# Placing ScalarE's share of a recurrence, a pooling stage's first splits and a w_a operand by ordering edges

## The chip, the cores and the metric

The kernel runs on one NeuronCore of a Trainium2 chip. The metric is the device time of one execution in microseconds (us), from start to end. Five engines work beside each other, each through its own instructions in order: TensorE (PE, with its weight loads shown as PEld), VectorE (DVE), ScalarE (ACT), GpSimd (POOL), and SyncE (SP), which here only issues DMA transfers. A time of this kernel is told apart from another when the two differ by about 0.2%, or 3 us.

## What is computed

One decoder block on 1024 tokens of width 1024, in float32. Its core, cut from the reference:

```python
proj = x @ w_in                     # -> q | f | i | og | pool_v | gate_a | gate_b, 1024 columns each
f = lb + (1 - lb) * sigmoid(f_pre);  k = 1 - f;  q = silu(q) * 128 ** -0.5
# per head of 128:  S_t = diag(f_t) S_{t-1} + k_t i_t^T,   o_t = S_t^T q_t
o = o * rsqrt(mean(o ** 2) + eps) * hgrn_norm_g * sigmoid(og)
a = o @ w_a
b = per_group_linear(causal_mean_w(pool_v) - pool_v, w_pool) * pool_scale
x = LN(alpha * x + (sigmoid(gate_a) * a + sigmoid(gate_b) * b) @ w_out)
x = LN(alpha * x + relu(x @ w_up) ** 2 @ w_down)
```

## The kernel before

**Products.** Every large product is cut Strassen-fashion into seven products of halves of 512 (`pair`, L267). One such product is 12 matmuls of 128x512 (`prod`, L207 to L215): four pieces of the contraction, each with high by high (L212), high by low (L214) and low by high (L215), because each operand is held as a high and a low part. A weight tile `raw` that DMA brought is split when it is needed: ScalarE writes the high part `w<-raw` (L126), VectorE subtracts it for the low one (L127). Results collect in four PSUM banks `ps_pj`; a bank is given back when ScalarE has copied it (`copied`, L275, into a tile `c`, `f` or `q`) or VectorE has added it (`added`, L279). Sigmoids of gates and of recurrence inputs (L690, L697, L717, L733) are ScalarE's too.

**The recurrence.** Between 115 us and 600 us the products of `x @ w_in` run, and the recurrence of eight heads in two halves of 512 tokens runs beside them. TensorE's order is fixed by hand there (`ORDER`, L33, and `turning`, L377): behind each product the recurrence takes one turn, 8.25 turns for one of the 16 halves. In the first turn of a half stand the outputs of the half before (L1025, L1027), and on ScalarE their squares (L1031), a root (L1032, which loads a function table first) and four scalings by it (L1035); then the transposed keys (L964, their copy L966) and the scores of this half (L971, L982) in the PSUM bank `sc`. In the turns behind it the next half is prepared by pieces (`prepare`, L890): running products on VectorE (L897 to L905), k = 1 - f on ScalarE (L909), products on VectorE (L935, L937), two ScalarE copies (L940, L943) with VectorE's other halves of them, three VectorE products (L946 to L949), and two more ScalarE copies (L953, L955) into `q64` and `k64`, which the last scores (L982) read. In the fourth turn the scaled outputs are transposed (L1041).

**The pooling stage and w_a.** When the recurrence's inputs are all made, the loop over `POOL_AFTER` (L1096) sets the pooling's products (`pool_products`, L746; L113 to L115 in one of two banks `ps_tr`) between the products of the last two gate pairs. w_pool's four groups are loaded into one tile `tC` (L763) in turn and split (L768) into `tD`, `tE`, `tF` and `og`, their inputs `po` in L769. For each product a gate tile `f<-gb` is loaded (ring of four tiles, L784), multiplied with the bank (L791) and stored as `pb<-f` (L792); the last two instead are copied out by ScalarE (L789). Then comes `a = o @ w_a`: `o_operand` (L628) loads four tiles `c<-o` for "a11" (L635) and splits each (ScalarE L131, VectorE L132).

**Who sets the order.** TensorE's is written out in this stretch; the order of ScalarE, VectorE, GpSimd and SP is chosen when the program is built, by a scheduler that simulates the engines. `tc.issue_after(x)` gives it an ordering edge: what is issued inside goes behind x on x's own engine, or behind x's issue, without a semaphore.

Of the kernel before, what the change touches and what calls it, by code (L numbers as in the profile page):

```python
# [28 lines left out]
NW = 10  # L29
PER_HALF = 8.25  # L30
TURN_BACK = 4
TURNS_AHEAD = 3
ORDER = (  # L33
    ("inputs", 1), ("pooled", 0), ("inputs", 2), ("gates", 0), ("output_gates", 2), ("inputs", 3), ("pooled", 1),
# [17 lines left out]
def tile_hybrid_block(  # L52
# [189 lines left out]
    def w_tile():  # L242
        return wq.tile([P, CH, P], F32R, tag="w", name=nm("w"), bufs=NW)

    def w_part(src):
        return split(src, w_tile)

    n_c = [0]

# [17 lines left out]
    def pair(raw, rooms, takes, pz_tag="pj", twin=False, pc_tag="pj", turned=False):  # L267
# [4 lines left out]

        def copied(room, ps):
            t = room()
            A.copy(t, ps)  # L275
            return t

        def added(t, ps):
# [375 lines left out]
    with tc.tile_pool(name="tmp", bufs=1, side="right", reuse_waits="tile") as tmp:  # L654
# [25 lines left out]
        def head_inputs(h, behind=()):  # L680
            fs, qs = inputs[h] = [None, None], [None, None]

            def room_f():
                fs[1] = tt("f")
                return fs[1]

            def take_f(u):
                def take(src):
                    t = fs[u] = fs[u] or tt("f")
                    A.activation(t, src, AF.Sigmoid)  # L690
                    A.activation(t, t, AF.Identity, bias=lb[:, h : h + 1], scale=one_lb[:, h : h + 1])
                return take

            def take_q(u):
                def take(src):
                    t = qs[u] = tt("q")
                    A.activation(t, src, AF.Sigmoid)  # L697
# [14 lines left out]
        def output_gates(h):  # L712

            def take(dst, src=False):
                def put(t):
                    s = c_late() if src else t
                    A.activation(s, t, AF.Sigmoid)  # L717
                    nc.sync.dma_start(out=dst, in_=s)
                return put

            run(pair(
                loaded_blocks(w_in, 3 * D + h * P, 3 * D + (h + 1) * P), (c_soon, c_late, c_late),
                (take(ogd[h][0]), take(ogd[h + 1][0], True), take(ogd[h][1]), take(ogd[h + 1][1])),
            ))

        def gates(j):
            final = j == KT - 1
            room = (lambda: tt("q")) if final else c_late

            def take(dst, src=None, u=None):  # L730
                def put(t):
                    s = (tt("og") if final else c_late()) if src else t
                    A.activation(s, t, AF.Sigmoid)  # L733
# [10 lines left out]
        held = [None, None]  # L744

        def pool_products():  # L746

# [16 lines left out]
                return raw, [loaded(pod[2 * g + i][u], pod_tile) for i in range(2)]  # L764

            def parts(g, u, raw, pods):
                if raw is not None:
                    w_parts[g] = split(raw, lambda: wide(w_tiles(F32R)))  # L768
                return [split(t, row_tile) for t in pods]  # L769

            w_parts = {}
            todo = [(g, u) for g in range(CH) for u in range(2)]
# [3 lines left out]
            for n, (g, u) in enumerate(todo):  # L776
                if n + 2 < len(todo):
                    soon.append(load(*todo[n + 2]))
                wh, wl = w_parts[g]
                for i in (0, 1) if g < CH - 1 else (1, 0):  # L780
                    w = slice(i * P, (i + 1) * P)
                    j = 2 * g + i
                    final = j == KT - 1
                    t = tt("v") if final else loaded(gbd[j][u], lambda: tt("f"))  # L784
                    ps = ps_tile("tr", 2)
                    mm3(ps, [(wh[:, c, w], wl[:, c, w], *pl[c]) for c in range(2)])
                    if final:
                        held[u] = t
                        A.activation(t, ps, AF.Copy, scale=pscale[:, j : j + 1])  # L789
# [95 lines left out]
        class Half:  # L885
# [4 lines left out]
            def prepare(self):  # L890
# [14 lines left out]
                V.tensor_tensor_scan(  # L905
                    to_end[:, QUARTER - 1 :: -1], ft[:, QUARTER : 0 : -1], first_of, 0.0, ALU.mult, ALU.max,
                )
                k = ft
                A.activation(k, ft, AF.Identity, bias=cmask[:, P - 1 : P], scale=-1.0)  # L909
# [23 lines left out]
                G.tensor_mul(ek[:, :, 0], p64[:, :, 1], p32[:, :, 1])  # L933
                yield
                V.tensor_mul(q, q, fd)  # L935
                self.kr = kr = tt("tE")
                V.tensor_mul(kr, k, to_end)  # L937
                yield
                self.kc = kc = tt("tD")
                A.copy(pairs_of(kc)[:, :, 0], pairs_of(kr)[:, :, 0])  # L940
                V.tensor_mul(pairs_of(kc)[:, :, 1], pairs_of(kr)[:, :, 1], bc(rT2[:, :, 1], [P, NB // 2, SUB]))
                self.qc = qc = tt("tF")
                A.copy(pairs_of(qc)[:, :, 1], pairs_of(q)[:, :, 1])  # L943
# [6 lines left out]
                yield  # L950
                self.q64 = q64 = hgp.tile([P, CH, 2, 32], F32, tag="q64", name=nm("q64"))
                self.k64 = k64 = hgp.tile([P, CH, 2, 32], F32, tag="k64", name=nm("k64"))
                A.copy(q64[:, :, 0], half64(q, 1)[:, :, 0])  # L953
                V.tensor_mul(q64[:, :, 1], half64(q, 1)[:, :, 1], bc(p32[:, :, 2], [P, CH, 32]))
                A.copy(k64[:, :, 1], half64(kr, 0)[:, :, 1])  # L955
                V.tensor_mul(k64[:, :, 0], half64(kr, 0)[:, :, 0], bc(p32[:, :, 1], [P, CH, 32]))
                self.q = q

# [60 lines left out]
            def outputs(self):  # L1019
# [11 lines left out]
                    A.activation(on[:, chunk(c)], o[:, chunk(c)], AF.Square, accum_out=ss[:, c : c + 1])  # L1031
                A.activation(ss, ss, AF.Sqrt, bias=eps_rms, scale=1.0 / P)  # L1032
                V.reciprocal(ss, ss)
                for c in range(CH):
                    A.activation(on[:, chunk(c)], o[:, chunk(c)], AF.Copy, scale=ss[:, c : c + 1])  # L1035

            def turn_outputs(self):

# [7 lines left out]
        def recurrence():  # L1046
# [10 lines left out]
            for n in range(2 * HEADS + 1):  # L1057
# [483 lines left out]
```

## Time and profile before

| | |
|---|---|
| median of 3 runs | 1460.81 us (1459.44 to 1462.52) |
| the profiled execution | 1460.42 us |
| its span, first to last instruction | 1458.7 us (1.7 us lie outside it) |
| granted TensorE clock, mean | 0.996 |
| VectorE busy | 1100.4 us (75%) |
| ScalarE busy | 759.3 us (52%) |
| chain of work that ended last | PE 86%, DVE 7%, DMA 3%, ACT 2% |
| 115 to 600 us: TensorE busy | 478.13 of 485.00 us |
| 600 to 665 us: TensorE busy | 59.08 of 65.00 us, DMA share 0.87 |
| 665 to 850 us: TensorE busy | 185.00 of 185.00 us |

How to read it: a row of a timeline has the start, the duration, the engine, the line of the kernel, the operation, what it writes and reads, and in brackets the idle time of the engine ahead of it with what ended that. Matmuls are pipelined, so one of 128x512 lasts 0.39 us and the next starts 0.227 us behind it. A view of waits lists, for each waiting line, what it waited for, the total in us, the number of times and the longest.

### The profile page before, as it was taken

What the parts mean: (1) busy time and instruction counts of PE and PEld (TensorE: products, weight loads), DVE (VectorE), ACT (ScalarE), POOL (GpSimd) and SP (SyncE); (2) the same over time, 40 slices, a digit from 0 to 9 for tenths busy, and PEclk for the clock granted to TensorE, in tenths of its full rate; (3) what the DMA queues carried; (4) which work ended last, traced back from release to release, by engine and by line L of the source; (5) the groups of instructions that cost most, each with busy time, mean ns of one, the idle gap of its engine ahead of it and who ended that gap; (6) DMA issues with size and microseconds to landing.
All of it is one profiled execution on the core that took longest, in us unless ns stands there. A gap on an engine that the chain in (4) does not pass through costs nothing.

```text
span 1458.7 us, 20882 instructions
## 1 busy us (share of the span) xinstructions
PE 1433.3 (98%) x7377; PEld 1188.7 (81%) x7377; DVE 1100.4 (75%) x1807; ACT 759.3 (52%) x1383; POOL 106.7 (7%) x288
## 2 busy tenths in 40 slices
PE   9999999999999999989999999999999999999997
PEld 7888888888887887868888888888888888888886
DVE  6968878888697795579885598666666787777877
ACT  5445567566656655556442366555555443333535
POOL 0002112112212110000002100000000100000000
PEclk9999999999999999999999999999999999999999
DMA  7242344444454455689463125444447774445322
GB/s 267 65 130 88 99 125 138 123 112 143 110 133 127 123 132 169 192 315 354 135 231 111 68 92 188 158 144 154 146 162 262 281 253 156 148 141 171 121 73 115
DMA packets 187161, 228.15 MB, mean 156 GB/s; under 512 B 12176, under 2 KB 110512, under 8 KB 187056
## 3 DMA queue, kind: packets, MB, share of 16 engines
q1 hardware_dynamic: 181088, 212.91, 44.0%
q0 software_dynamic: 5184, 11.54, 4.1%
q10 hardware_dynamic: 784, 2.38, 0.5%
q8 instruction: 58, 0.95, 0.3%
q14 instruction: 47, 0.39, 0.1%
HBM read 149.70 MB, written 77.07 MB: 155 GB/s over the span
## 4 chain that ended last, share of the span: by engine, by line
PE 86%; DVE 7%; DMA 3%; ACT 2%; issue 1%; SPq 0%; DVEq 0%; ACTq 0%
PE ps_pj L212 14%; PE ps_pj L215 14%; PE ps_pj L214 14%; PE ps_pj L1423 4%; PE ps_pj L1424 4%; PE ps_pj L1422 4%; PE ps_pj L114 2%; PE ps_pj L115 2%; PE ps_pj L113 2%; PE ps_tr L1423 1%; PE ps_tr L1424 1%; PE ps_tr L1422 1%; DVE w L127 1%; PE ps_hg L212 1%; PE ps_sc L215 1%
## 5 line engine op out<-in xcount | busy, mean ns | idle before, releaser
L212 PE MATMUL ps_pj<-act,w 128*128 128x512 f32 x1068 | 422.2, 395 | 12.4 <-ACT c L275 5.6
L215 PE MATMUL ps_pj<-act,w 128*128 128x512 f32 x1068 | 416.7, 391 | 0.6 <-DVE w L127 0.6
L214 PE MATMUL ps_pj<-act,w 128*128 128x512 f32 x1068 | 416.6, 391 | 0.0
L126 ACT CAST w<-raw 128x512 fp32r<-128x512 f32 x311 | 192.9, 622 | 272.0 <-PE ps_pj L214 184.0
L127 DVE TENSOR_TENSOR w<-raw,w 128x512 fp32r<-128x512 f32 x311 | 213.0, 687 | 102.2 <-ACT w L126 100.8
L212 PEld LDWEIGHTS ps_pj<-act,w 128*128 128x128 f32 x1068 | 201.3, 188 | 58.0 <-ACT c L275 7.4
L215 PEld LDWEIGHTS ps_pj<-act,w 128*128 128x128 f32 x1068 | 201.2, 188 | 44.7 <-DVE w L127 1.8
L214 PEld LDWEIGHTS ps_pj<-act,w 128*128 128x128 f32 x1068 | 201.3, 188 | 40.7
L1384 ACT CAST act<-act 128x1024 fp32r<-128x1024 f32 x66 | 66.9, 1050 | 109.0 <-issue 35.0
L1424 PE MATMUL ps_pj<-act,act 128*128 128x512 f32 x240 | 93.0, 389 | 0.0
L1423 PE MATMUL ps_pj<-act,act 128*128 128x512 f32 x240 | 93.0, 389 | 0.0
L1385 DVE TENSOR_TENSOR act<-act,act 128x1024 fp32r<-128x1024 f32 x66 | 79.5, 1221 | 17.8 <-ACT act L1384 17.8
L1422 PE MATMUL ps_pj<-act,act 128*128 128x512 f32 x240 | 92.5, 389 | 0.0
L279 DVE TENSOR_TENSOR c<-c,ps_pj 128x512 f32<-128x512 f32 x91 | 62.1, 682 | 31.0 <-PE ps_pj L215 30.6
L275 ACT COPY c<-ps_pj 128x512 f32<-128x512 f32 x92 | 53.5, 582 | 3.0 <-PE ps_pj L215 1.7
L1422 PEld LDWEIGHTS ps_pj<-act,act 128*128 128x128 f32 x240 | 45.0, 188 | 9.4
L1423 PEld LDWEIGHTS ps_pj<-act,act 128*128 128x128 f32 x240 | 45.0, 188 | 9.4
L1424 PEld LDWEIGHTS ps_pj<-act,act 128*128 128x128 f32 x240 | 45.0, 188 | 9.3
L284 DVE TENSOR_TENSOR raw<-raw,raw 128x512 f32<-128x512 f32 x43 | 29.6, 689 | 30.5 <-DMA raw<-in_w_in_dram 28.6
L1293 ACT ACTIVATE c<-c 128x512 f32<-128x512 f32 x61 | 38.6, 633 | 1.7
L1292 ACT ACTIVATE c<-c 128x512 f32<-128x512 f32 x46 | 29.1, 632 | 15.6 <-DVE c L279 15.5
L1378 DVE TENSOR_TENSOR act<-act,ps_pj 128x512 f32<-128x512 f32 x45 | 30.2, 683 | 5.4 <-PE ps_pj L1424 5.1
(415 smaller groups left out, 2683.5 us busy)
## 6 DMA issues: line engine op xcount, KB each, us to landing
h<-c SPq DMA_DIRECT2D x106, 256.0 KB, 2.8
raw<-in_w_in_dram SPq DMA_DIRECT2D x100, 256.0 KB, 3.1
act<-h SPq DMA_DIRECT2D x78, 256.0 KB, 3.0
draw<-in_w_down_dram SPq DMA_DIRECT2D x16, 1024.0 KB, 7.8
raw<-in_w_up_dram SPq DMA_DIRECT2D x56, 256.0 KB, 2.9
hf<-h SPq DMA_DIRECT2D x34, 256.0 KB, 2.9
s<-og POOLq DMA_DIRECT2D x28, 256.0 KB, 6.2
v<-v SPq DMA_DIRECT2D x16, 256.0 KB, 3.2
```

Of the source, the lines that this page charges most:

```text
L126: A.copy(hi, src)
L127: V.tensor_sub(lo, src, f(hi))
L212: PE.matmul(ps, wh[:, k], th, start=first and k == 0, stop=False, skip_group_check=True)
L214: PE.matmul(ps, wh[:, k], tl, start=False, stop=False, skip_group_check=True)
L215: PE.matmul(ps, wl[:, k], th, start=False, stop=k == CH - 1, skip_group_check=True)
L275: A.copy(t, ps)
L279: V.tensor_add(t, t, ps)
L1384: A.copy(hi, src)
L1385: V.tensor_sub(lo, src, f(hi))
L1422: PE.matmul(ps, hh[:, w], wh, start=fresh and n == 0, stop=False, skip_group_check=True)
L1423: PE.matmul(ps, hh[:, w], wl, start=False, stop=False, skip_group_check=True)
L1424: PE.matmul(ps, hl[:, w], wh, start=False, stop=n == M - 1, skip_group_check=True)
```

## The change

1. `noted` remembers the last bank copy (`copied`) or sigmoid that was issued, and everything that the recurrence asks of ScalarE is put behind it (`behind_act`): k = 1 - f (L909), the copies of L940, L943, L953, L955, and the four scalings of L1035. k = 1 - f is also written one piece later, and the scalings become a function of their own, `scale_outputs`, which is called in the turn behind the root (`TURN_SCALE = 1`) and not with it.
2. `w_part` keeps each weight split's two instructions; `behind_weight` puts w_pool's parts and their inputs' behind the last weight split written so far.
3. The loads of operand a11 are put behind the last load of a gate tile `f<-gb`, and its splits behind the fourth last weight split.

No instruction is added or removed on any engine.

```diff
 def w_part(src):
-    return split(src, w_tile)
+    hi, lo = w_tile(), w_tile()
+    hi_of.append(A.copy(hi, src).ins)
+    lo_of.append(V.tensor_sub(lo, src, f(hi)).ins)
+    return hi, lo
+
+@contextmanager
+def behind_weight(n=-1):
+    with tc.issue_after(hi_of[n]), tc.issue_after(lo_of[n]):
+        yield
+
+def noted(i):
+    last_act[0] = i.ins
+    return i
+
+def behind_act():
+    return tc.issue_after(last_act[0])
...
-            A.copy(t, ps)
+            noted(A.copy(t, ps))
...
             def parts(g, u, raw, pods):
-                if raw is not None:
-                    w_parts[g] = split(raw, lambda: wide(w_tiles(F32R)))
-                return [split(t, row_tile) for t in pods]
+                with behind_weight():
+                    if raw is not None:
+                        w_parts[g] = split(raw, lambda: wide(w_tiles(F32R)))
+                    return [split(t, row_tile) for t in pods]
...
-                    t = tt("v") if final else loaded(gbd[j][u], lambda: tt("f"))
+                    t = tt("v") if final else tt("f")
+                    if not final:
+                        last_gate[0] = nc.sync.dma_start(out=t, in_=gbd[j][u]).ins
...
-                k = ft
-                A.activation(k, ft, AF.Identity, bias=cmask[:, P - 1 : P], scale=-1.0)
...
                 V.tensor_mul(q, q, fd)
+                k = ft
+                with behind_act():
+                    A.activation(k, ft, AF.Identity, bias=cmask[:, P - 1 : P], scale=-1.0)
...
-                A.copy(q64[:, :, 0], half64(q, 1)[:, :, 0])
+                with behind_act():
+                    A.copy(q64[:, :, 0], half64(q, 1)[:, :, 0])
...
-                for c in range(CH):
-                    A.activation(on[:, chunk(c)], o[:, chunk(c)], AF.Copy, scale=ss[:, c : c + 1])
+                self.o, self.root = o, ss
+
+            def scale_outputs(self):
+                with behind_act():
+                    for c in range(CH):
+                        w = chunk(c)
+                        A.activation(self.on[:, w], self.o[:, w], AF.Copy, scale=self.root[:, c : c + 1])
...
                 for turn in range(1, round(at) - round(at - PER_HALF)):
+                    if turn == TURN_SCALE and old:
+                        old.scale_outputs()
                     if turn == TURN_BACK:
...
-        o_operand("a11")
+        with tc.issue_after(last_gate[0]), behind_weight(-4):
+            o_operand("a11")
```

What that moves, at three places. In the rows the number behind a name tells tiles apart; lines are those of each kernel's own text (L126, L275, L909, L953, L955, L1032 and L1035 of before are L250, L294, L958, L979, L982, L1059 and L1068 after the change; L131, L789, L635 and L623 for a gate tile are L132, L811, L654 and L806).

ScalarE behind the root of the outputs at 444.76 us of the trace (`c_897` is the copy of the bank `ps_pj_883`). Before:

```order
L1032 ACT_TABLE_LOAD
L1032 ACTIVATE ss_891_4843<-ss_891_4843,eps_rms_82 128x4
L909 ACTIVATE f_873_4778<-f_873_4778,cmask_79 128x512
L1035 ACTIVATE tH_892_4844<-ps_hg_890_4835,ss_891_4843 128x128 x4
L126 COPY w_930_5056<-raw_925_5047 128x512
L275 COPY c_897_4908<-ps_pj_883_4800 128x512
```

After the change:

```order
L1059 ACT_TABLE_LOAD
L1059 ACTIVATE ss_891_4843<-ss_891_4843,eps_rms_82 128x4
L250 COPY w_930_5056<-raw_925_5047 128x512
L294 COPY c_897_4904<-ps_pj_883_4800 128x512
L1068 ACTIVATE tH_892_4844<-ps_hg_890_4835,ss_891_4843 128x128 x4
L250 COPY w_934_5078<-raw_926_5049 128x512
```

The weight's high part and the bank copy moved ahead of the scalings and of k = 1 - f, which now stands six rows behind the scalings. The same happens behind the root at 304.44 us.

ScalarE ahead of a score at 495.6 us (`q64_994` and `k64_995` are what L982 of before reads; `c_993` is the copy of bank `ps_pj_983`). Before, the two copies stood thus, some 15 rows ahead of the bank copy `c_993`:

```order
L940 COPY tD_985_5346<-tE_968_5275 128x16x16
L126 COPY w_987_5352<-raw_977_5320 128x512
L953 COPY q64_994_5393<-q_870_4756 128x4x32
L275 COPY f_952_5201<-ps_pj_936_5082 128x512
L955 COPY k64_995_5394<-tE_968_5275 128x4x32
```

After the change:

```order
L752 ACTIVATE c_984_5344<-c_984_5344 128x512
L250 COPY w_1029_5579<-raw_1024_5570 128x512
L294 COPY c_993_5391<-ps_pj_983_5331 128x512
L979 COPY q64_994_5393<-q_870_4756 128x4x32
L982 COPY k64_995_5394<-tE_968_5275 128x4x32
```

They moved behind the bank copy. VectorE's products of the same half (L946, L947, L949 and L956 of before) moved likewise, to just ahead of the addition of `c_984`.

ScalarE at 640 us (`act_1360` and `act_1362` are parts of operand a11, `v_1330` is the pooling's product `ps_tr_1331` copied out, `w_1311` a weight of the last gate pair). Before, with `v_1330` twenty-one rows behind the first of these:

```order
L131 COPY act_1360_7108<-c_1361_7109 128x512
L126 COPY w_1311_6882<-raw_1292_6820 128x512
L275 COPY q_1299_6844<-ps_pj_1298_6831 128x512
L126 COPY w_1323_6930<-tA_1301_6848 128x512
L126 COPY w_1325_6934<-tA_1302_6850 128x512
L131 COPY act_1362_7113<-c_1363_7114 128x512
```

After the change:

```order
L250 COPY w_1338_6986<-raw_1293_6822 128x512
L132 COPY act_1360_7108<-c_1361_7109 128x512
L294 COPY q_1329_6956<-ps_pj_1298_6831 128x512
L132 COPY act_1362_7113<-c_1363_7114 128x512
L811 ACTIVATE v_1330_6958<-ps_tr_1331_6959,prm_120 128x512
L132 COPY act_1364_7118<-c_1365_7119 128x512
```

The parts of a11 moved behind the split of `w_1338`, two gate products later, and two of them now stand ahead of the copying out of `ps_tr_1331`. Their loads on SP moved too. After the change SP's rows there read (`f_1343` is the last gate tile):

```order
L806 DMA f_1332_6967<-gb6_0_963 128x512
L806 DMA f_1343_7016<-gb6_1_964 128x512
L755 DMA ga7_0_949<-q_1299_6844 128x512
L654 DMA c_1361_7109<-o0_0_903 128x512
L814 DMA pb4_1_992<-f_1317_6904 128x512
L654 DMA c_1363_7114<-o1_0_905 128x512
```

Before, the load of `c_1361` stood ahead of the last six gate tiles' loads.

Likewise w_pool's first parts (`tD_1213<-tC_1208`), which stood just behind the scalings at 554.99 us, now stand behind the split of `w_1205`, which ran at 578.49 us.

More of the change, by code (lines that the diff above doesn't have):

```diff
@@ L31 @@
 TURN_BACK = 4
+TURN_SCALE = 1
 TURNS_AHEAD = 3
@@ L243, in w_tile @@
         return wq.tile([P, CH, P], F32R, tag="w", name=nm("w"), bufs=NW)
+    hi_of, lo_of, last_act = [], [], [None]
     def w_part(src):
-        return split(src, w_tile)
+        hi, lo = w_tile(), w_tile()
[11 more added lines that the diff above has]
+        return tc.issue_after(last_act[0])
     n_c = [0]
@@ L690, in take @@
                     A.activation(t, src, AF.Sigmoid)
-                    A.activation(t, t, AF.Identity, bias=lb[:, h : h + 1], scale=one_lb[:, h : h + 1])
+                    noted(A.activation(t, t, AF.Identity, bias=lb[:, h : h + 1], scale=one_lb[:, h : h + 1]))
                 return take
@@ L696, in take @@
                     t = qs[u] = tt("q")
-                    A.activation(t, src, AF.Sigmoid)
+                    noted(A.activation(t, src, AF.Sigmoid))
                     V.scalar_tensor_tensor(t, src, QSCALE, t, ALU.mult, ALU.mult)
@@ L716, in put @@
                     s = c_late() if src else t
-                    A.activation(s, t, AF.Sigmoid)
+                    noted(A.activation(s, t, AF.Sigmoid))
                     nc.sync.dma_start(out=dst, in_=s)
@@ L732, in put @@
                     s = (tt("og") if final else c_late()) if src else t
-                    A.activation(s, t, AF.Sigmoid)
+                    noted(A.activation(s, t, AF.Sigmoid))
                     if final and u is not None:
@@ L742, in gates @@
             ))
-        held = [None, None]
+        held, last_gate = [None, None], [None]
         def pool_products():
@@ L939, in prepare @@
                 self.kc = kc = tt("tD")
-                A.copy(pairs_of(kc)[:, :, 0], pairs_of(kr)[:, :, 0])
+                with behind_act():
+                    A.copy(pairs_of(kc)[:, :, 0], pairs_of(kr)[:, :, 0])
                 V.tensor_mul(pairs_of(kc)[:, :, 1], pairs_of(kr)[:, :, 1], bc(rT2[:, :, 1], [P, NB // 2, SUB]))
                 self.qc = qc = tt("tF")
-                A.copy(pairs_of(qc)[:, :, 1], pairs_of(q)[:, :, 1])
+                with behind_act():
+                    A.copy(pairs_of(qc)[:, :, 1], pairs_of(q)[:, :, 1])
                 V.tensor_mul(pairs_of(qc)[:, :, 0], pairs_of(q)[:, :, 0], bc(rT2[:, :, 0], [P, NB // 2, SUB]))
@@ L952, in prepare @@
                 self.k64 = k64 = hgp.tile([P, CH, 2, 32], F32, tag="k64", name=nm("k64"))
-                A.copy(q64[:, :, 0], half64(q, 1)[:, :, 0])
+                with behind_act():
+                    A.copy(q64[:, :, 0], half64(q, 1)[:, :, 0])
                 V.tensor_mul(q64[:, :, 1], half64(q, 1)[:, :, 1], bc(p32[:, :, 2], [P, CH, 32]))
-                A.copy(k64[:, :, 1], half64(kr, 0)[:, :, 1])
+                with behind_act():
+                    A.copy(k64[:, :, 1], half64(kr, 0)[:, :, 1])
                 V.tensor_mul(k64[:, :, 0], half64(kr, 0)[:, :, 0], bc(p32[:, :, 1], [P, CH, 32]))
@@ L1033, in outputs @@
                 V.reciprocal(ss, ss)
-                for c in range(CH):
-                    A.activation(on[:, chunk(c)], o[:, chunk(c)], AF.Copy, scale=ss[:, c : c + 1])
+                self.o, self.root = o, ss
+            def scale_outputs(self):
+                with behind_act():
+                    for c in range(CH):
+                        w = chunk(c)
+                        A.activation(self.on[:, w], self.o[:, w], AF.Copy, scale=self.root[:, c : c + 1])
             def turn_outputs(self):
```

## The prediction

> **What bounds the kernel now.** I read the page's head first, then its costliest groups, then the view of waits of TensorE, and after that timelines around each wait. Page and waits:
>
> ```profile
> span 1458.7 us, 20882 instructions
> PE 1433.3 (98%) x7377; PEld 1188.7 (81%) x7377; DVE 1100.4 (75%) x1807; ACT 759.3 (52%) x1383; POOL 106.7 (7%) x288
> ```
>
> ```profile
> PE ps_pj L212 <- ACT c L275: 5.6, 3, 3.1
> PE ps_pj L212 <- ACT w L126: 5.3, 1, 5.3
> PE ps_pj L212 <- ACT f L275: 0.8, 1, 0.8
> PE ps_pj L215 <- DVE w L127: 0.6, 2, 0.5
> PE ps_pj L212 <- DVE c L279: 0.6, 1, 0.6
> ```
>
> TensorE is busy 98% of the span. The change doesn't touch its instructions, so it can win only these waits, 5.6 + 5.3 + 0.8 + 0.6 + 0.6 = 12.9 us, and what follows a wait. ScalarE is 52% busy, so work is late there by its place in the queue and not for want of time. The question is then, for each wait, what the copy or split that ends it was queued behind, and whether the moved work is itself in time.
>
> **The change part by part.** All starts are on the trace's own time. Matmuls of a block start 0.23 us apart (635.76 and 635.99 in the rows of the stretch from 636 us), so a wait's price is the distance of the two starts around it less 0.23.
>
> *The wait at 446 us.* ScalarE, then TensorE:
>
> ```profile
> 444.76 0.30 ACT L1032 ACTIVATE ss<-ss,eps_rms 128x4 f32<-128x4 f32 x1
> 445.65 0.72 ACT L909 ACTIVATE f<-f,cmask 128x512 f32<-128x512 f32 x1 [0.59 <-DVE tC L905]
> 446.56 1.14 ACT L1035 ACTIVATE tH<-ps_hg,ss 128x128 f32<-128x128 f32 x4 [0.19 <-DVE ss L1033]
> 447.58 0.63 ACT L126 CAST w<-raw 128x512 fp32r<-128x512 f32 x1
> 448.08 0.61 ACT L275 COPY c<-ps_pj 128x512 f32<-128x512 f32 x1
> ```
> ```profile
> 446.12 0.39 PE L215 MATMUL ps_pj<-act,w 128*128 128x512 f32 x1
> 448.75 0.50 PE L212 MATMUL ps_pj<-act,w 128*128 128x512 f32 x1 [2.24 <-ACT c L275]
> 449.09 0.40 PE L214 MATMUL ps_pj<-act,w 128*128 128x512 f32 x1
> ```
>
> The bank copy ended at 448.69 and TensorE began the next block at 448.75, 448.75 - 446.12 - 0.23 = 2.4 us late, and 0.1 more at the restart. Ahead of the copy stood k = 1 - f and the scalings, both waiting for VectorE. After the change the split and the copy come right behind the root: the root ends at 445.06, the split takes about 0.5 to the next start, the copy ends at about 446.2. The bank is wanted at 446.35. **-2.5 us.** What is late next is the scalings, three rows further on; the transposes that read them (L1041) stand in the fourth turn, so they cost nothing as long as they lose under 3 us, by my reading of the order.
>
> *The wait at 308 us* is that for `f` in the view of waits, 0.8, and has the same form: the bank copy behind root, k = 1 - f and scalings. With 0.1 at the restart: **-0.9 us**.
>
> *The wait at 558 us.*
>
> ```profile
> 560.33 0.62 ACT L126 CAST tD<-tC 128x512 fp32r<-128x512 f32 x1 [4.20 <-DMA tC<-in_w_pool_dram]
> 561.37 0.58 ACT L275 COPY c<-ps_pj 128x512 f32<-128x512 f32 x1
> ```
> ```profile
> 558.47 0.39 PE L215 MATMUL ps_pj<-act,w 128*128 128x512 f32 x1
> 562.00 0.50 PE L212 MATMUL ps_pj<-act,w 128*128 128x512 f32 x1 [3.14 <-ACT c L275]
> ...
> 563.93 0.63 PE L212 MATMUL ps_pj<-act,w 128*128 128x512 f32 x1
> ...
> 566.45 0.40 PE L212 MATMUL ps_pj<-act,w 128*128 128x512 f32 x1
> ```
>
> ScalarE stood 4.20 us before w_pool's first split, for a load, with a bank copy behind it. TensorE restarts 562.00 - 558.47 - 0.23 = 3.3 us late. Then its matmuls last 0.63 us for a while and not 0.39: the twelve from 562.00 to 566.45 take 4.45 where 12 x 0.23 = 2.76 are due, 1.7 more. After the change the w_pool split stands behind a weight split that ran at about 578 us, and the bank copy behind the root, done by 556 us, where it is wanted at 558.7. The first pooling product begins at 605 us, so the split has over 20 us left. **-5.0 us.** [...] Here the rows decide: matmuls last 0.63 behind 3.14 us of idle time, and 0.40 at once behind the 2.24 us that end at 448.75.
>
> *The stretch from 636 us.* ScalarE, TensorE and SP:
>
> ```profile
> 640.46 0.62 ACT L131 CAST act<-c 128x512 fp32r<-128x512 f32 x1 [7.80 <-DMA c<-o]
> ...
> 653.98 0.69 ACT L789 ACTIVATE v<-ps_tr,prm 128x512 f32<-128x512 f32 x1
> ```
> ```profile
> 635.76 0.39 PE L114 MATMUL ps_tr<-w,tD 128*128 128x512 f32 x1
> 635.99 0.39 PE L115 MATMUL ps_tr<-w,tE 128*128 128x512 f32 x1
> 641.65 0.80 PE L212 MATMUL ps_pj<-act,w 128*128 128x512 f32 x1 [5.27 <-ACT w L126]
> 646.00 0.39 PE L113 MATMUL ps_tr<-w,tD 128*128 128x512 f32 x1
> ...
> 657.87 0.40 PE L113 MATMUL ps_tr<-w,tF 128*128 128x512 f32 x1
> ```
> ```profile
> 638.33 0.55 SPq L623 DMA_DIRECT2D f<-gb  x1
> ```
> ```profile
> f<-gb SPq DMA_DIRECT2D x14, 256.0 KB, 3.1
> pb<-f SPq DMA_DIRECT2D x14, 256.0 KB, 4.7
> c<-o SPq DMA_DIRECT2D x12, 256.0 KB, 4.7
> ```
>
> a11's first part waited 7.80 us for its load, and the weight split that TensorE needs stood behind it: 641.65 - 635.99 - 0.23 = 5.4 late, then a block of 4.35 (to 646.00) for 2.76, 1.6 more, and the 0.5 of L127's wait shortly behind: 7.5 us to win. But only if nothing takes its place before the pooling product at 657.87, which would then be due at 650.4. That product takes the bank that L789 copies out, and after the change two parts of a11 stand ahead of L789, whose loads stand behind the last gate tile's. That load is paced by its ring of four tiles: the last but four was issued at 638.33, landed 3.1 later (641.4), is multiplied in some 0.75 and stored in 4.7 (646.9), so the last can leave at about 647; the store of a gate and a11's two loads follow within 1.4 us, the second lands 4.7 later, at 653.1. Its split (0.62) and L789 (0.69) end at 654.4. The product restarts there, 657.87 - 654.4 = 3.5 earlier than before, not 7.5: **-3.5 us**. The bounds are 0, where loads land no sooner than now, and -7.5, where they land some 4 us sooner than the rows' medians. I take the rows' medians.
>
> *New waits.* VectorE first. At 404 us TensorE waits 0.6 for a bank that VectorE adds (`c` by L279 in the view of waits). VectorE's groups, with their mean duration in ns:
>
> ```profile
> L817 DVE TENSOR_TENSOR pC<-pA 128x269 f32<-128x269 f32 (+1 forms) x32 | 13.8, 430 | 0.3
> ...
> L949 DVE TENSOR_TENSOR tC<-tE,ek 128x512 f32<-128x512 f32 x16 | 10.9, 682 | 0.1
> ...
> L956 DVE TENSOR_TENSOR k<-tE,p 128x128 f32<-128x128 f32 x16 | 4.5, 282 | 0.0
> ```
>
> Behind one another they cost about 0.35, 0.6 and 0.2, since the next starts some 0.08 before the end. In the new order four pooling operations of the first size have come ahead of that addition, and two recurrence products, of the last size (L954) and the second (L995), have gone behind it: 4 x 0.35 - 0.8 = 0.6 longer. **+0.6 us** (from -0.7, all of the wait and its restart, to +1.4). Second, the half scored at 495.6 us:
>
> ```profile
> 490.96 0.69 DVE L284 TENSOR_TENSOR raw<-raw,raw 128x512 f32<-128x512 f32 x1 [4.16 <-DMA raw<-in_w_in_dram]
> ```
> ```profile
> 475.77 0.30 ACT L955 COPY k<-tE 128x128 f32<-128x128 f32 x1
> ```
> ```profile
> 496.27 0.68 PE L982 MATMUL sc<-q,k 128*64 128x64 f32 x8
> ```
>
> Before, `k64` was written 20 us ahead of the scores that read it. The bank copy behind which it goes:
>
> ```profile
> 494.06 0.58 ACT L275 COPY c<-ps_pj 128x512 f32<-128x512 f32 x1
> ```
>
> Now four products of VectorE (L946 and L947 of about the first size, L949, L956: 1.5 us) stand behind L284, which waits for a load, and ahead of the addition L279 of `c_984`; sigmoid and bank copy follow the addition, and `q64` and `k64` the copy. The copy would start at 495.6, the two copies end at 496.7: **+0.5 us**. In the other 15 halves the same reading of the new order against before's times leaves 1 to 10 us; I cost them at nothing, and at 1 us each where the cover is gone.
>
> *The sum:* -2.5 - 0.9 - 5.0 - 3.5 + 0.6 + 0.5 = -10.8 us. The profiled execution took 1460.42, of which 1.7 lie outside the span; that is 0.4 below the median of the runs and inside their spread. 1460.42 - 10.8 = 1449.6.
>
> **The rivals.** *All waits go.* For it: the bank copies and splits do stand ahead of everything that waits, and the loads' medians hide a spread of some us. Against it: two parts of a11 now ahead of L789. 2.5 + 0.9 + 5.0 + 7.5 + 0.7 = 16.6 less: 1443.8.
>
> *The gate ring gives all back at 636 us.* The stretch's wait moves from a weight split to a bank `ps_tr`, at the same length. For it: SP issues in order, and a11's loads now stand behind the last gate tile's. Then the sum is -10.8 + 3.5 = -7.3, and the time 1453.1. [...]
>
> *Slower: the recurrence's preparation comes too late.* The mechanism is the half at 495.6 us in all halves. Its last copies stand behind bank copies that wait for VectorE's additions, and VectorE's own products wait in turn for ScalarE's k = 1 - f and stand ahead of later additions and subtractions. It decides where `k64` ends after L982's start, so from a delay of 1 to 10 us that the order does not show. At the 1.5 us of that half's VectorE work for each of 16 halves that is 24 us more: 1460.42 - 10.8 + 24 = 1473.6; the sign turns at 0.7 us a half. For it: 20 us of margin were spent. Against it: ScalarE is 52% busy, and its longest block of table load, root and scalings is under 4 us.
>
> *The change doesn't do what it says.* The waits would stay, if the copies were held by something else than the work ahead of them. The rows speak against it: each late copy started at the end of the row ahead of it. 1460.4.
>
> **How the numbers follow.** Forecast (1447 to 1452): 0.46. All waits go: 0.12. The ring gives back (1452 to 1457): 0.22. No change: 0.07. Late preparation, slower: 0.13. The predicted time is 1449.6. The range is 1443.5 to 1457: it takes in the first three, 0.80, and with them the bounds of the stretch at 636 us (-7.5 to 0) and of the addition at 404 us. This kernel's runs can tell 0.2%, 2.9 us: faster than 1457.9 has 0.46 + 0.12 + 0.22 = 0.80, within it 0.07, slower 0.13.
>
> **What would show it.** In the changed profile the waits of L212 for `c` and `f` by L275 and for `w` by L126 are gone, and no matmul near 562 and 642 us lasts 0.63. The pooling product that was at 657.87 waits for L789, 2 to 5 us. At the score near 495 us stands a wait of about 0.5 for `k` or `q`. I would be wrong if scores or transposes (L971, L982, L1041) wait at many halves, if banks wait for L279 for several us, or if the first products of w_a wait for a11 or a12, whose loads come some 12 us later.

## The result, and the profile after

| | before | after |
|---|---|---|
| median | 1461.66 us (1459.44 to 1462.74, 4 runs) | 1451.79 us (1448.97 to 1453.22, 4 runs) |
| the profiled execution, its span | 1460.42, 1458.7 us | 1451.65, 1449.9 us |

The ratio is 0.9932, with a 95% interval of 0.9912 to 0.9952. The change is faster, by 9.9 us between the medians and by 8.8 us between the two profiled spans; 1449.6 was forecast. The head of the page after and its view of TensorE's waits:

```profile
span 1449.9 us, 20883 instructions
PE 1429.3 (99%) x7377; PEld 1186.5 (82%) x7377; DVE 1100.0 (76%) x1807; ACT 757.0 (52%) x1383; POOL 104.0 (7%) x288
```
```profile
PE ps_tr L114 <- DVE f L813: 2.5, 2, 1.5
PE ps_pj L213 <- DVE c L298: 2.3, 3, 1.0
PE ps_tr L114 <- ACT v L811: 2.2, 1, 2.2
PE ps_sc L171 <- DMA x<-in_x_dram: 1.9, 1, 1.9
...
PE ps_pj L213 <- ACT c L294: 0.2, 1, 0.2
```

Against the five rows of before (L213 here is L212 of before, L114 here is L113): the 5.6 and 0.8 us for ScalarE's bank copies have become 0.2, and the 5.3 us for a weight split is gone. In their place stand waits for the pooling's gate products (L813, L791 of before) and for the copying out of a pooling product (L811, L789 of before), and the waits for VectorE's additions (L298, L279 of before) have grown from 0.6 to 2.3. The wait for x is the first load of the program, which the change doesn't touch; it was 0.9 in the execution of before.

How the bank copies came free, on ScalarE of after:

```profile
441.85 0.30 ACT L1059 ACTIVATE ss<-ss,eps_rms 128x4 f32<-128x4 f32 x1
443.37 0.62 ACT L250 CAST w<-raw 128x512 fp32r<-128x512 f32 x1 [1.23 <-PE ps_pj L215]
443.90 0.58 ACT L294 COPY c<-ps_pj 128x512 f32<-128x512 f32 x1
445.25 1.14 ACT L1068 ACTIVATE tH<-ps_hg,ss 128x128 f32<-128x128 f32 x4 [0.76 <-DVE ss L1060]
```

Split and copy follow the root and wait only for TensorE; the scalings come behind them and wait for VectorE alone.

A landmark shows where the 8.8 us of span were won. The last pooling product ahead of the stretch at 636 us began at 634.73 before and at 628.29 after: 6.4 sooner. The pooling product that was at 657.87 is at 648.96: 8.9 sooner. From there to the end nothing more moved. So 6.4 us were won up to the stretch and 2.5 in it.

What is left in the stretch is longest at L811, the copying out of a pooling product. ScalarE of after shows what stands ahead of it:

```profile
645.88 0.62 ACT L132 CAST act<-c 128x512 fp32r<-128x512 f32 x1 [4.21 <-DMA c<-o]
...
647.70 0.62 ACT L132 CAST act<-c 128x512 fp32r<-128x512 f32 x1 [0.71 <-DMA c<-o]
648.23 0.68 ACT L811 ACTIVATE v<-ps_tr,prm 128x512 f32<-128x512 f32 x1
```

Two parts of a11 wait 4.21 and 0.71 us for their loads; L811 follows and ends at 648.91, and the matmul that needs its bank begins at 648.96.

### The profile page after: what moved, and what is told of

Its sections match the earlier page's. It is cut to its first block, busy times and chain, and to the rows that moved or that the text cites. A ratio compares the mean times of both kernels' runs of the same rounds, so it can differ in the third digit from the quotient of the medians.

```text
span 1449.9 us, 20883 instructions
## 1 busy us (share of the span) xinstructions
PE 1429.3 (99%) x7377; PEld 1186.5 (82%) x7377; DVE 1100.0 (76%) x1807; ACT 757.0 (52%) x1383; POOL 104.0 (7%) x288
## 4 chain that ended last, share of the span: by engine, by line
PE 91%; DVE 5%; DMA 2%; ACT 1%; issue 1%; SPq 0%; DVEq 0%; ACTq 0%
PE ps_pj L213 15%; PE ps_pj L215 15%; PE ps_pj L216 15%; PE ps_pj L1458 4%; PE ps_pj L1460 4%; PE ps_pj L1459 4%; PE ps_pj L114 2%; PE ps_pj L115 2%; PE ps_pj L116 2%; PE ps_tr L1458 1%; PE ps_tr L1460 1%; PE ps_tr L1459 1%; PE ps_hg L215 1%; PE ps_hg L213 1%; PE ps_sc L215 1%; PE ps_hg L216 1%
## 5 line engine op out<-in xcount | busy, mean ns | idle before, releaser
L213 PE MATMUL ps_pj<-act,w 128*128 128x512 f32 x1068 | 420.5, 394 | 2.6 <-DVE c L298 2.3
L250 ACT CAST w<-raw 128x512 fp32r<-128x512 f32 x303 | 187.6, 621 | 273.9 <-PE ps_pj L215 196.2
L251 DVE TENSOR_TENSOR w<-raw,w 128x512 fp32r<-128x512 f32 x303 | 206.8, 686 | 96.1 <-ACT w L250 92.1
L213 PEld LDWEIGHTS ps_pj<-act,w 128*128 128x128 f32 x1068 | 200.5, 188 | 47.4 <-DVE c L298 4.1
L298 DVE TENSOR_TENSOR c<-c,ps_pj 128x512 f32<-128x512 f32 x91 | 62.1, 683 | 37.4 <-PE ps_pj L216 36.6
L294 ACT COPY c<-ps_pj 128x512 f32<-128x512 f32 x92 | 53.5, 581 | 3.5 <-PE ps_pj L216 2.2
L303 DVE TENSOR_TENSOR raw<-raw,raw 128x512 f32<-128x512 f32 x43 | 29.6, 687 | 22.1 <-DMA raw<-in_w_in_dram 18.3
L668 POOL DMA_DIRECT2D s<-og x28 | 24.9, 1162 | 138.7 <-DVE og L1076 138.7
```

What stands on the lines that cost most here:

```text
L213: PE.matmul(ps, wh[:, k], th, start=first and k == 0, stop=False, skip_group_check=True)
L250: hi_of.append(A.copy(hi, src).ins)
L251: lo_of.append(V.tensor_sub(lo, src, f(hi)).ins)
L294: noted(A.copy(t, ps))
L298: V.tensor_add(t, t, ps)
```

## The experiments

The ratio of each kernel is against runs of before of the same round, whose medians were 1462.72 to 1462.89 us. Kernels of different rounds are better compared by their ratios or the spans of their profiles than by the microseconds of their medians.

**One part at a time.** The theory was that each part of the change takes away its own waits. The first kernel has the recurrence part alone:

```diff
-                with behind_weight():          # w_pool's parts
...
-        with tc.issue_after(last_gate[0]), behind_weight(-4):
-            o_operand("a11")
+        o_operand("a11")
```

> The recurrence part alone (k = 1 - f, the four copies and the scalings behind the last bank copy or sigmoid; pooling parts and a11 as before). Theory (each part takes away its own waits, and the moved VectorE products add about 0.4 + 0.3 + 0.5 + 1.1 us at 404, 493, 499 and 544 us): TensorE's waits of 0.9 at 308 us and 2.4 at 446 us are gone, those of 3.3 (and 1.7 of slow matmuls) at 558 us and of 5.4 (and 1.6) at 636 us stay, the four new waits are there; about 1.0 us below before, 1460. Rival (the waits at 558 and 636 us hang on the same crowding of ScalarE by the recurrence): those shrink too, and the time is over 5 us below before.

Measured: 1455.26 us, ratio 0.9962 (0.9942 to 0.9982), span 1453.4. The waits at 308 and 446 us are gone, as expected. Of the four new waits that were expected, those for additions at 403 and 543 us have come, 1.1 us each with the restart, and those at 493 and 499 us have not. Neither theory had the wait at 558 us right: it is gone, and that at 636 us is not.

```profile
PE ps_pj L213 <- ACT w L250: 5.3, 2, 5.0
PE ps_pj L213 <- DVE c L298: 2.0, 2, 1.0
```

Why the wait at 558 us went, ScalarE and SP of this kernel show:

```profile
555.08 0.62 ACT L127 CAST tD<-tC 128x512 fp32r<-128x512 f32 x1 [2.47 <-DMA tC<-in_w_pool_dram]
...
556.13 0.58 ACT L294 COPY c<-ps_pj 128x512 f32<-128x512 f32 x1
```
```profile
550.12 1.21 SPq L642 DMA_DIRECT2D tC<-in_w_pool_dram  x1
```

w_pool's split still stands ahead of the bank copy, but it waits 2.47 us and not 4.20, because the scheduler has put its load one row further ahead on SP (550.12; before, at 555.82, behind a weight's load). The scalings' 1.1 us that stood ahead of it are behind the copy too. The copy ends at 556.7, 0.2 us late.

The pooling part alone:

```diff
-        return tc.issue_after(last_act[0])
+        return nullcontext()            # and k = 1 - f and the scalings where they were
...
+        o_operand("a11")                # without the two edges
```

> The pooling part alone (w_pool's parts and their inputs' behind the last weight split; the recurrence and a11 as before). Theory: the wait at 558 us and its slow matmuls go, 5.0 us, those at 308, 446 and 636 us stay, none is new at 499 or 544 us: 1456 to 1457. Rival (the bank copy at 558 us is then held by the scalings and the root): a wait of over 1 us stays there and the gain is under 4.

Measured: 1456.83 us, ratio 0.9961 (0.9946 to 0.9976), span 1452.0. The theory holds at 558 us:

```profile
PE ps_pj L213 <- ACT w L250: 3.5, 1, 3.5
PE ps_pj L213 <- ACT c L294: 3.1, 2, 2.9
```

The 2.9 is the wait at 446 us; there is none left at 558 us, and none at 544. One of 0.4 us for an addition stands at 503 us, where before was 0.2 us late. At 636 us the weight split's wait is 3.5 and not 5.3, with slow matmuls of 1.9 us behind it. The theory did not have that: the order on SP changed there too, and the first load of a11 left at 627.50, where it left at 635.50 before.

The a11 part alone (the recurrence as above, w_pool's parts without their edge):

> The a11 part alone (a11's loads behind the last gate tile's load, its splits behind the fourth last weight split; all else as before). Theory (the wait for a weight split turns into waits for gate tiles and for the copying out of a pooling product that stands behind a11's splits): the waits at 308, 446 and 558 us stay, that of 5.4 at 636 us goes with its slow matmuls, 1.7 + 1.2 + 2.3 us of new ones for L813 and L811's like stand in its place, 2.5 us gained: 1459. Rival (the parts need each other): no gain or a loss of some us at 636 to 660 us.

Measured: 1463.37 us, ratio 0.9993 (0.9975 to 1.0012), span 1459.0: no gain that shows. TensorE's waits:

```profile
PE ps_pj L213 <- ACT c L294: 6.4, 3, 3.5
PE ps_tr L114 <- DVE f L812: 3.6, 2, 2.0
PE ps_tr L114 <- ACT v L810: 1.8, 1, 1.8
```

The weight split's wait has turned into three others, 5.4 us together, and slow matmuls of 1.4 us follow the second. (L812 and L810 are L813 and L811 of after.) What the rival said came true here: TensorE loses 7.8 us in the stretch, as much as in before, so by itself this part gives back what it takes. This profile also began some 2 us late, at the first loads, so its span understates it a little.

The reverse, after without its a11 part, says more of that part's worth, since the edges of recurrence and pooling stand as after:

```diff
-        with tc.issue_after(last_gate[0]), behind_weight(-4):
-            o_operand("a11")
+        o_operand("a11")
```

> After the change without its a11 part: recurrence and pooling parts alone. Theory (from the part alone, which won nothing: the gate tiles' ring and the pooling copy give back what the weight split's wait cost): the stretch at 630 us has a wait of some 3.5 us for a weight split and 1.6 of slow matmuls in place of 1.7 + 1.2 + 2.3, and the time is within 1 us of after's, 1451.8. Rival (the a11 part is worth the 2.5 us that the stretch won): 1454.3.

Measured: 1455.00 us, ratio 0.9944 (0.9929 to 0.9959), span 1452.9, so 3 us above after in the medians and the spans: the rival is nearer. By the ratios it is 1.8 us, and their intervals overlap, so that this difference is likely and not shown by the times alone. In the profile TensorE waits 4.8 us for a weight split at 636 us and loses 2.6 us to slow matmuls behind it, 7.7 with the restart, where after loses 5.5 in that stretch: some 2 us are the a11 part's. Another 1.4 us of the difference lie at a score:

```profile
PE ps_pj L213 <- ACT w L250: 4.8, 1, 4.8
...
PE sc L1009 <- ACT k L982: 1.6, 1, 1.6
```
```profile
488.98 0.69 DVE L303 TENSOR_TENSOR raw<-raw,raw 128x512 f32<-128x512 f32 x1 [5.63 <-DMA raw<-in_w_in_dram]
...
491.67 0.68 DVE L298 TENSOR_TENSOR c<-c,ps_pj 128x512 f32<-128x512 f32 x1
```
```profile
493.43 0.58 ACT L294 COPY c<-ps_pj 128x512 f32<-128x512 f32 x1
...
494.10 0.30 ACT L982 COPY k<-tE 128x128 f32<-128x128 f32 x1
```

This is the half of the forecast's new wait (L983 of VectorE, L979 and L982 of ScalarE are L956, L953 and L955 of before). A weight's load came late, VectorE stood 5.63 us before the operation that reads it (L303), and all that is behind it, addition, bank copy and `k64`, went late in turn. After stood 4.20 us there and the score began 0.2 us late; the kernel further down with the stores alone stood 3.25 us, and its score is on time.

**Who makes VectorE's additions late.** With the restart after waits 1.1 us at 403, 0.5 at 499 and 1.1 at 544 us for additions, and 0.2 at 493 us for `k64`. This kernel frees the four copies and keeps the edges of scalings and k = 1 - f:

```diff
-                with behind_act():
-                    A.copy(q64[:, :, 0], half64(q, 1)[:, :, 0])
+                A.copy(q64[:, :, 0], half64(q, 1)[:, :, 0])     # and kc, qc, k64 likewise
```

> After the change, with the four copies (kc, qc, q64, k64) no longer put behind a bank copy or sigmoid; scalings, k = 1 - f, pooling and a11 parts as after. Theory (the waits for additions at 403, 499 and 544 us and for k64 at 493 us come from those copies and the VectorE products beside them having moved late): they fall to 0.7 at 403 us and to nothing at the others, 2.4 us less than after, 1449.4; no wait returns at 308 and 446 us. Rival 1 (k = 1 - f being late moves the VectorE products, whatever the copies do): the waits stay and the time is that of after, 1451.8. Rival 2 (the copies themselves held bank copies before): waits of 0.5 us and more come back for L294 and the time is above after's.

Measured: 1451.98 us, ratio 0.9925 (0.9895 to 0.9954), span 1450.1: the time of after. Yet not by the first rival's way:

```profile
PE ps_tr L114 <- ACT v L811: 2.3, 1, 2.3
PE ps_tr L114 <- DVE f L813: 2.2, 2, 1.8
...
PE ps_pj L213 <- DVE c L298: 1.0, 2, 0.6
PE ps_pj L213 <- ACT c L294: 0.5, 2, 0.3
```

The additions' waits fell from 2.3 to 1.0: that at 544 us and that for `k64` are gone, that at 403 us is halved, that at 499 us is 0.3 longer. A wait for a bank copy of 0.3 came back at 445 us. The waits at 403 and 544 us are 1.1 to 1.3 us in every kernel here whose copies keep the edges, and 0.5 and nothing in the two that free them, so the copies' lateness does make these two. It is not shown for the other two: at 499 us and for `k64` three kernels with the edges have no wait. About 1.3 us were won in the recurrence; they were lost again behind the wait of 2.3, where eight matmuls lasted 0.63 us in this execution and cost 1.6.

**What holds the stretch at 636 us.** Three kernels vary a11. In the first only its splits keep an edge:

```diff
-        with tc.issue_after(last_gate[0]), behind_weight(-4):
-            o_operand("a11")
+        o_operand("a11")                 # its split_into behind behind_weight(-4), its loads free
```

> After the change, with only a11's splits behind the fourth last weight split and its loads free, as before the change. Theory (the wait of 2.2 us at 649 us comes from a11's loads standing behind the last gate tile's, so that ScalarE waits for them ahead of the copying out of the pooling product): with the loads issued some 10 us sooner the wait goes, 2.3 us less than after, 1449.5. Rival (SP issues in order, and a11's loads ahead of gate tiles' make these late): the waits for L813 of 1.5 and 1.0 us grow by what is won, and the time is that of after, 1451.8.

Measured: 1450.43 us, ratio 0.9913 (0.9898 to 0.9928), span 1447.9.

```profile
PE ps_tr L114 <- DVE f L814: 2.9, 2, 2.6
...
PE ps_pj L213 <- DVE q L298: 0.6, 1, 0.6
```

The wait for the pooling copy is gone, as the theory said; the gate tiles' waits (L814 here is L813 of after) grew from 2.5 to 2.9 and 0.6 came for an addition, the rival's way but less than half of its size. The intervals of this ratio and after's overlap, so a gain of 1.4 us against after is likely and not shown.

In the second a11's splits go behind the pooling product's copy as well:

```diff
-        with tc.issue_after(last_gate[0]), behind_weight(-4):
+        with tc.issue_after(last_gate[0]), behind_weight(-4), tc.issue_after(held_by[0]):   # the copy L811
             o_operand("a11")
```

> After the change, with a11's splits also put behind ScalarE's copying out of the pooling product whose bank TensorE waits for at 649 us. Theory (only their place ahead of it on ScalarE makes that wait): it goes, nothing else changes, 2.3 us less, 1449.5, and the first products of w_a find a11 in time. Rival (a11 is then late for w_a): a wait of 2 us for an operand part at about 655 us takes its place.

Measured: 1451.97 us, ratio 0.9920 (0.9903 to 0.9936), span 1450.8: nothing won.

```profile
PE ps_tr L114 <- DVE f L813: 2.3, 2, 2.0
...
PE ps_pj L216 <- DVE w L251: 1.4, 1, 1.4
PE ps_pj L213 <- ACT w L250: 0.9, 1, 0.9
```

The wait for L811 went and 1.4 + 0.9 came for weight splits, which now stand behind a11's parts. On ScalarE those parts waited 2.72 and 2.11 us for loads just ahead of the split that TensorE waits 0.9 us for. So the theory fails, and waits of the rival's size came, though for weight splits and not for an operand part: the wait moved with the parts, and what is late is the loads.

The third keeps that and takes the stores of the pooling's products out of SP's queue:

```diff
-                        nc.sync.dma_start(out=pbd[j][u], in_=t)
+                        nc.gpsimd.dma_start(out=pbd[j][u], in_=t)
```

> As with a11's splits behind the pooling product's copy, and the pooling's stores issued from GpSimd and not from SP. Theory (the waits of 1.5 and 1.0 us for L813 are SP's: it stands before a gate tile's load until a store has landed, with stores of other tiles queued behind it): they go too, 2.5 us more, 1447. Rival (the ring of four tiles with stores of 4.7 us and loads of 3.1 us is the limit, whoever issues): they stay, 1449.5; stores from GpSimd take longer to land (6.2 us for s<-og), and they could grow by 1 to 2 us, 1451.

Measured: 1445.17 us (1444.53 to 1447.11), ratio 0.9880 (0.9865 to 0.9894), span 1443.9. That is 6.8 us below the kernel without the moved stores, and the theory had 2.5: the waits for weight splits went as well as those for L813. Nothing between 546 and 857 us makes TensorE wait 0.2 us or more:

```profile
PE ps_pj L213 <- DVE c L298: 2.3, 3, 1.0
...
PE sc L1009 <- ACT k L982: 0.3, 1, 0.3
```

SP's issues, and one gate product of VectorE, show what did it, first of after, then of this kernel:

```profile
635.38 1.60 SPq L806 DMA_DIRECT2D f<-gb  x2
637.07 0.86 SPq L814 DMA_DIRECT2D pb<-f  x2
638.49 0.74 DVE L813 SCALAR_TENSOR_TENSOR f<-ps_tr,prm,f 128x512 f32<-128x512 f32 x1
640.53 0.92 SPq L806 DMA_DIRECT2D f<-gb  x2
...
641.97 0.42 SPq L654 DMA_DIRECT2D c<-o  x1
642.49 0.38 SPq L814 DMA_DIRECT2D pb<-f  x1
```
```profile
626.90 7.11 SPq L806 DMA_DIRECT2D f<-gb  x4
...
635.49 0.32 SPq L806 DMA_DIRECT2D f<-gb  x1
635.86 3.00 SPq L654 DMA_DIRECT2D c<-o  x6
```

In after SP stands before the loads of 635.38 and 640.53 until a tile of the ring is free (6.0 us of waits for `pb<-f` to land, from 632 to 645 us), and the stores that free others stand behind those loads. The gate product that begins at 638.49 is done at 639.23, and its store leaves only at 642.49; over the 14 stores of after this delay has a median of 3.1 us and reaches 7.8. With all 14 stores on GpSimd none stands among SP's loads. So the loads leave as tiles come free, and a11's first one 6 us sooner. The transfers themselves became no faster: this kernel's median from issue to landing is 4.4 us for `f<-gb` (after 3.1) and 4.6 for `pb<-f` (after 4.0).

The stores by themselves, on after:

> After the change with the pooling's stores issued from GpSimd and nothing else. Theory (SP's order is the limit of the stretch: with the stores out of its queue gate tiles and a11 come some 6 us sooner, so that a11's place ahead of the pooling copy costs nothing): no wait over 0.5 us from 625 to 665 us and 1445 to 1446. Rival (a11's place on ScalarE holds the pooling product's copy all the same): a wait of 1 us or more for L811 stays near 649 us, 1447 or above.

Measured: 1446.95 us (1445.27 to 1448.82), ratio 0.9884 (0.9869 to 0.9899), span 1443.2. In the stretch only this is left:

```profile
PE ps_tr L114 <- ACT v L811: 0.3, 1, 0.3
```

The median lies above the theory's 1445 to 1446 and at the rival's bound, so the time doesn't tell them apart; the wait does, and the theory's mechanism holds: a11's place ahead of the pooling copy costs 0.3 us once its loads come in time, and the stores' queue was the cause of all three waits. And the stores by themselves on before:

> Before the change with the pooling's stores issued from GpSimd and nothing else. Theory (the waits of before at 308, 446 and 558 us have nothing to do with these stores, and that of 5.4 at 636 us is a load of a11 queued late on SP behind the ring): 5.4 and its 1.6 of slow matmuls shrink to under 2, the others stay, 1454 to 1456. Rival (the split of a weight stands behind a11's part on ScalarE, and its load comes late whoever stores): the wait stays over 4 us and the time over 1459.

Measured: 1460.17 us, ratio 0.9982 (0.9966 to 0.9998), span 1456.1. The median is the rival's, over 1459. The profiled execution took 1457.77, one of the faster, and its waits fall between the two theories:

```profile
PE ps_pj L212 <- ACT c L275: 4.7, 3, 2.5
PE ps_pj L212 <- DVE c L279: 2.8, 2, 2.2
PE ps_pj L212 <- ACT w L126: 2.8, 1, 2.8
```

The wait for the weight split is 2.8 and not 5.3, and has no slow matmuls behind it. Against that an addition is waited for 2.2 us at 502 us, with 1.7 of slow matmuls, far from the stores. Moving the stores is worth some 5 us on after (4.8 between the medians, 4.9 in the stretch itself, 6.7 between the spans, where waits elsewhere differ too) and about 2.6 on before.

**A version that beats both.** Stores from GpSimd, a11 behind the pooling copy, and the four copies free:

> Stores from GpSimd and a11 behind the pooling copy, and the four copies of the recurrence no longer put behind a bank copy or sigmoid. Theory (in the recurrence freeing the copies takes away 1.1 at 544, 0.5 at 493 and half of 1.1 at 403 us and brings 0.4 at 445 and 0.3 more at 499 us, as in the run without it at the stores): 1.0 to 1.5 us less than with the stores alone, 1444. Rival (the new order of the scheduler gives other waits of the same size): no difference that shows, 1445.

Measured: 1444.81 us (1443.62 to 1445.67), ratio 0.9869 (0.9854 to 0.9883), span 1443.8: the span of the kernel with the stores and without the free copies was 1443.9, so freeing the copies shows no gain here, the rival's case. Additions are waited for 1.5 us and not 2.3 and the 0.3 for `k64` is gone, but bank copies are waited for 1.0 us and not 0.2. Against before this is 1.3% off the time, about twice what the change itself gave.

## Why the prediction was right or wrong

The time of 1451.79 us is 2.2 above the forecast of 1449.6 and inside its range. Term by term:

1. *The wait at 446 us, -2.5.* Right in place and size: copy and split stand behind the root and the wait is gone. The kernel with the recurrence part alone shows that this part did it.
2. *The wait at 308 us, -0.9.* Right, for the same reason: it is gone in the kernel with the recurrence part alone and stays, at 0.7, in the one with the pooling part alone.
3. *The wait at 558 us, -5.0 with its slow matmuls.* Right in size. The cause given, that the copy is no longer behind w_pool's split, is one of two that do it: the recurrence part alone takes nearly all of that wait away too, by an earlier load and by the scalings behind the copy. And 1.7 of the 5.0 are slow matmuls that are no fixed price of that wait: in the kernel with the a11 part alone the wait stood there still, at 3.45 us, and no slow matmul followed.
4. *The stretch at 636 us, -3.5.* The landmark says -2.5. The mechanism came as forecast: TensorE waits 2.2 us for L811, which stands behind two parts of a11, which wait for loads behind the last gate tile's. L811 ended at 648.9, which is 655.3 on the time of before (6.4 had been won ahead of it), where 654.4 was forecast. What failed is the reason for the lateness. The prediction said that a ring of four tiles, with a store of 4.7 and a load of 3.1 us, sets the pace. The three kernels that have the change and the stores on GpSimd have the same ring with transfers no faster, and at most 0.3 us of wait. It is SP's order that set the pace: the prediction let a store leave as soon as its product is done, and in after it stood 3.1 us, in the median, behind loads. That the last gate load left as forecast (641.13, which is 647.5 on the time of before, where about 647 was forecast) is partly luck: the store that freed its tile left 0.8 us late, which the forecast did not have, and took 3.6 us where it had 4.7.
5. *The addition at 404 us, +0.6.* Measured +0.4: 1.1 against 0.7 with the restart. The recurrence part alone has the same 1.1, and with the copies free it is 0.5. That the four pooling operations now ahead of it make it, as the forecast's sum has it, was not tried by itself.
6. *The half scored at 495 us, +0.5.* Measured +0.2 in after, and 0 to 1.6 from kernel to kernel among those with the same edges, with the lateness of one weight's load. The mechanism is right where that load is late, and the size goes with it.
7. *The other halves at nothing.* This term was mis-sized. The scores did stay covered; but additions were waited for 0.5 us at 499 us (0.2 in before, at 502) and 1.1 at 544 us, where VectorE's moved products stand ahead of an addition just as at 404 us. That is +1.4 that the prediction had at nothing. The 1.1 at 544 us is there in every kernel whose copies keep the edges; the 0.5 is missing in three of them.

With 0.4 of the first loads, which the change doesn't touch, the terms give -2.5 - 0.9 - 5.0 - 2.5 + 0.4 + 0.2 + 1.4 + 0.4 = -8.5; the span moved by 8.8. Against the forecast's -10.8 the largest misses are 1.0 in the stretch and 1.4 in the other halves.

Of the rivals, "all waits go" fails on points 4, 5 and 7. "The ring gives all back" came true in part: 7.5 us were to be won and 2.5 were. "Late preparation" is real as a mechanism but took about 2 us in all, not 24. The medians from issue to landing were 3.1 us for the gate loads and 4.0 for the stores in after, and the stretch is decided by the queue.

## What to carry to other kernels

A wait is removed by asking what stands ahead of the late instruction in its own queue and moving that, but the moved work has its own users on other engines: read the new order once for every bank, not only for those that waited before. Where loads and stores of one ring share an issuing queue, as on SP in after, look at what a load that waits for a free tile holds back: there it was the very stores that would free the next, which left 3.1 us behind their products in the median and up to 7.8. Taking these stores to another queue was worth some 5 us on the changed kernel, half of what the change itself gave, and about 2.6 us on the kernel before. And when a part alone wins nothing, try it again with the next limit removed before dropping it.

## What the runs showed of the hardware

In these runs the length of TensorE's wait alone does not tell whether slow matmuls come behind it. Of the two waits below, 2.18 and 2.25 us, one was followed by matmuls of 0.39 us and one by matmuls of 0.63. Where matmuls of before last 0.63, from 642 to 644 us behind the wait of 5.27, its granted clock is 0.50. After, then the kernel with the copies free:

```profile
648.96 0.50 PE L114 MATMUL ps_tr<-w,tF 128*128 128x512 f32 x1 [2.18 <-ACT v L811]
...
649.76 0.39 PE L114 MATMUL ps_tr<-w,tF 128*128 128x512 f32 x1
```
```profile
647.80 0.50 PE L114 MATMUL ps_tr<-w,tF 128*128 128x512 f32 x1 [2.25 <-ACT v L811]
...
648.63 0.63 PE L114 MATMUL ps_tr<-w,tF 128*128 128x512 f32 x1
```

In these traces the slow matmuls came behind single waits of 2.2, 2.25, 3.14, 3.49, 4.8, 5.0 and 5.3 us, and not behind others of 2.24, 2.49, 2.61, 2.75, 2.92 and even 3.45 us. In the kernel with the a11 part alone they came behind two waits of 1.6 and 2.0 us, 3.7 us apart. Where slow matmuls came they cost 1.4 to 2.6 us. What makes the difference was not tried.
